# Tiles between the stages of the long transforms: one channel's 32 values side by side instead of 128 channels side by side

## The chip, the cores and the metric

The kernel runs on one core of a Trainium2 chip. The metric is device time in microseconds for one execution; the kernel before was timed three times and the median is used. The engines are called PE (matmul; its weight load is a separate queue), DVE (vector), ACT (scalar), POOL (GpSimd) and SP (issues most transfers).

## The reference

One layer of an encoder block on 2048 tokens of width 1024, all in float32:

```
h = rmsnorm(x);  p = h @ W_in                      # 1024 -> 512 Fourier + 3 x 512 Hyena
y_f = rmsnorm(Re FFT2(positions, 64 channels of a group))     # 8 groups
y_h = rmsnorm(hyena(x1, x2, v)):
    u = short_conv(u)                              # 3 taps
    k = filters(positions)                         # small sine network, 2 orders x 512 channels
    z = v
    for n, gate in enumerate((x1, x2)):
        z = gate * (irfft(rfft(z, 4096) * rfft(k)[n])[:2048] + z * d[n])
x = x + concat(y_f, y_h) @ W_out
x = x + relu(rmsnorm(x) @ W_fc1)^2 @ W_fc2
out = rmsnorm(x)
```

The change concerns only the transforms: the Fourier mixing, the spectra of the filters `k`, and the two rounds of long convolution.

## The kernel before, in words

The program is one instruction stream per engine; the order in the code is, by engine, the order of execution, and engines meet through semaphores that the tile framework sets.

The stages in order: input projection (0 to about 410 us), Fourier mixing together with the generation of the first filters (410 to about 463), spectra of the filters (to about 656), the Hyena rounds (656 to 915), output projection, then the two layers of the MLP.

A transform of length 4096 (or 2048 in the Fourier part) is split in two factors. Positions are held as two digits; the first stage is a matmul over one digit, then a block transpose brings the other digit onto the partitions, and the second stage is a matmul for each of 32 frequencies. The block transpose is DVE's: it turns each 32x32 block, so the 32 values of one channel that lie on the free side go to 32 partitions, and what comes out is again 32 values for each channel. How these 32 values lie in memory is what changes.

*`fourier`.* For 16 groups of 16 channel pairs a matmul of 512 columns (L414) and a transpose into `G` (L415). Then for each of 17 frequencies up to four matmuls of 132 or 124 columns (L429 to L435) read row `f` of `G`. Between the steps of this generator the generation of filters is advanced.

*`filters`.* Eight units, for two orders and four blocks of 128 channels. `generate` makes the filter in eight steps (matmul L483, DVE's product with the decay L487, a split in a high and a low float32r part). `stage1` runs eight times for a unit: three float32r matmuls by `mm3` (L188 to L190) and a transpose into `Gk` (L535). `stage2` runs eight times: four matmuls of 128 columns with `Gk` as the moving operand (L540), a copy by ACT (L543), and every second time a store of the spectrum to DRAM. Steps of `generate` for the unit after next are put in between by the table `GENERATE`. The last units have no generation beside them.

*`hyena`.* Eight blocks, again two orders by four blocks of 128 channels, software-pipelined by hand. For a block:
- `first` (eight times): two matmuls of 256 columns from `zz` (L629), a transpose from PSUM into `G` (L630).
- `second` (eight times): four matmuls of 128 columns from `G` (L636); the product with the spectrum `ks`, which SP loads from DRAM (L615): ACT makes the swapped copy `zs` (L639, L640), DVE multiplies (L642), POOL multiplies (L643), POOL or DVE adds (L644).
- `inverse` (eight times): four matmuls (L652), and ACT's copy of the result into `V` (L653).
- `turn` (eight times): a transpose from `V` into `W` (L659), SBUF to SBUF.
- `gate` (four times): two matmuls of 512 columns on 64 output rows each, from `W` (L665), and DVE's product with the gate into `zz` (L666).

Block `i` runs its `second` while block `i-1` finishes `inverse` and is turned, block `i-2` is gated and block `i+1` does `first`. `LAG`, `TURNS`, `LAST` and `FIRSTS` fix this order.

All matmuls named here, but for those in `mm3`, are plain float32; the profile records each of them as two passes with a weight load each, so counts are twice those of the code. `pa` takes one of eight PSUM banks, each 512 float32 values wide.

Of the kernel before, what the change touches and what calls it, by code (L numbers as in the profile page):

```python
# [10 lines left out]
F32 = mybir.dt.float32  # L11
# [116 lines left out]
P = 128  # L128
# [6 lines left out]
def hybrid_block(ctx: ExitStack, tc: tile.TileContext, A, out):  # L135
    nc = tc.nc
# [27 lines left out]
    def pa(nm):  # L164
        return ps.tile([P, 512], F32, tag="a", name=nm, bufs=8)
# [241 lines left out]

    def fourier(fp, uf, e1f, ffs):
        groups = [(0,)] + [(f, f + 1) for f in range(1, 17, 2)]
        G = fp.tile([P, 32, 256], F32, tag="Gf", name="Gf")  # L410
        ufv = uf.rearrange("p t (b j) -> p t b j", b=2)
        for c in range(16):
            p = pa("pf1")
            nc.tensor.matmul(p, lhsT=e1f, rhs=ufv[:, :, :, 16 * c : 16 * c + 16], start=True, stop=True)  # L414
            nc.vector.transpose(G.rearrange("p f j -> p j f")[:, 16 * c : 16 * c + 16, :], p.rearrange("p (x j) -> p j x", j=16))  # L415
            yield

        def rows(i):

            n, p = len(groups[i]), pa("pf2")  # L420
            neg = fp.tile([P, 2, P], F32, tag="neg", name="neg", bufs=2)[:, 0:n]
            nc.scalar.mul(neg, ffs[i][:, :, 1], -1.0)
            for s, f in enumerate(groups[i]):
                co, si, ns = ffs[i][:, s, 0], ffs[i][:, s, 1], neg[:, s]
                a, b = p[:, 256 * s : 256 * s + 132], p[:, 256 * s + 132 : 256 * s + 256]
                gr, gi = (G[:, j].rearrange("p (c j) -> p c j", c=2) for j in (f, (16 + f) % 32))
                cos, sin = slice(0, 66), slice(66, 128)
                if f % 16 == 0:
                    nc.tensor.matmul(a, lhsT=co, rhs=gr[:, :, cos], start=True, stop=True)  # L429
                    nc.tensor.matmul(b, lhsT=ns, rhs=gr[:, :, sin], start=True, stop=True)  # L430
                else:
                    nc.tensor.matmul(a, lhsT=co, rhs=gr[:, :, cos], start=True, stop=False)
                    nc.tensor.matmul(a, lhsT=si, rhs=gi[:, :, cos], start=False, stop=True)
                    nc.tensor.matmul(b, lhsT=ns, rhs=gr[:, :, sin], start=True, stop=False)
                    nc.tensor.matmul(b, lhsT=co, rhs=gi[:, :, sin], start=False, stop=True)  # L435
            v = p.rearrange("p (s j) -> p s j", s=2)[:, 0:n]
            va = v[:, :, 0:132].rearrange("p s (c j) -> p s c j", c=2)
            sb = fp.tile([P, 2, 2, 62], F32, tag="sb", name="sb", bufs=2)[:, 0:n]
            nc.scalar.copy(sb, v[:, :, 132:256].rearrange("p s (c j) -> p s c j", c=2))

            row = fp.tile([P, 2, 388], F32, tag="row", name="row", bufs=2)[:, 0:n]

            def part(c, w):
                return row[:, :, c : c + 2 * w].rearrange("p s (c j) -> p s c j", c=2)

            nc.vector.tensor_add(part(0, 62), va[:, :, :, 0:62], sb)
            nc.vector.tensor_sub(part(132, 62), va[:, :, :, 0:62], sb)
            for c in (124, 256):
                nc.scalar.copy(part(c, 4), va[:, :, :, 62:66])
            nc.scalar.copy(row[:, :, 264:388], row[:, :, 0:124])  # L450
            nc.sync.dma_start(yfd[:, groups[i][0] : groups[i][0] + n, :], row)

        for i in range(len(groups)):
            rows(i)
            yield


    def filters(ctx, fp, gp, zp, zzs, norms, emb, wo, e1k, f2):
# [5 lines left out]
        class Unit:  # L464
# [62 lines left out]
            def stage1(self, c):  # L527
                if c == 0 and self is units[7]:

                    self.G = fp.tile([P, 32, 128], F32, tag="kh", name="Gk")  # L530
                elif c == 0:
                    self.G = gp.tile([P, 32, 128], F32, tag="Gk", name="Gk")
                p = pa("pk1")
                mm3(p, e1h, e1l, self.k[0][:, c], self.k[1][:, c], True, True)
                nc.vector.transpose(self.G.rearrange("p f c -> p c f")[:, 16 * c : 16 * c + 16, :], p.rearrange("p (l c) -> p c l", c=16))  # L535

            def stage2(self, q):
                p = pa("pk2")
                for j in range(4):
                    nc.tensor.matmul(p[:, 128 * j : 128 * j + 128], lhsT=f2[:, 4 * q + j, :], rhs=self.G[:, 4 * q + j, :], start=True, stop=True)  # L540
                if q % 2 == 0:
                    self.ks = sp.tile([P, 8, 128], F32, tag="ks", name="ks", bufs=3)
                nc.scalar.copy(self.ks[:, 4 * (q % 2) : 4 * (q % 2) + 4, :], p.rearrange("p (f c) -> p f c", f=4))  # L543
                if q % 2:
                    nc.sync.dma_start(kd[self.ct][self.n][:, 4 * q - 4 : 4 * q + 4, :], self.ks)
# [8 lines left out]
        sp = ctx.enter_context(pool("spectra", "right"))  # L554
# [4 lines left out]
        for i, u in enumerate(units):  # L559
# [12 lines left out]
            for q in range(8):  # L572
# [14 lines left out]
                j = 8 * i + q - 50  # L587
# [5 lines left out]
    def hyena(hp, wp, rp, zz, e1, b1, f2, a2, out_weights, out_ahead):  # L593
# [1 line left out]


        def big(nm):
            return (rp if nm == "W" else wp).tile([P, 32, 128], F32, tag=nm, name=nm, bufs=1 if nm == "W" else 2)

        class Block:  # L600
            def __init__(self, n, ct):
# [21 lines left out]
            def first(self, c):  # L623
                if c == 0:
                    self.G = big("G")
                p = pa("pz1")
                lo = 128 * self.ct + 16 * c
                for sp in range(2):
                    nc.tensor.matmul(p[:, 256 * sp : 256 * sp + 256], lhsT=e1[:, sp, :], rhs=zz[:, :, lo : lo + 16], start=True, stop=True)  # L629
                nc.vector.transpose(self.G.rearrange("p f c -> p c f")[:, 16 * c : 16 * c + 16, :], p.rearrange("p (l c) -> p c l", c=16))  # L630

            def second(self, q):
                ks = self.ahead if q == 0 and self.ahead else self.spectrum(q)
                p = pa("pz2")
                for j in range(4):
                    nc.tensor.matmul(p[:, 128 * j : 128 * j + 128], lhsT=f2[:, 4 * q + j, :], rhs=self.G[:, 4 * q + j, :], start=True, stop=True)  # L636
                p3 = p.rearrange("p (f c) -> p f c", f=4)
                zs = hp.tile([P, 4, 128], F32, tag="zs", name="zs", bufs=4)
                nc.scalar.mul(zs[0:64], p3[64:128], -1.0)  # L639
                nc.scalar.copy(zs[64:128], p3[0:64])  # L640
                y = hp.tile([P, 4, 128], F32, tag="y", name="y", bufs=5)
                nc.vector.tensor_mul(y, p3, ks[:, 0])  # L642
                nc.gpsimd.tensor_mul(zs, zs, ks[:, 1])  # L643
                (nc.gpsimd if self is not blocks[7] and q in (0, 1, 2, 3) else nc.vector).tensor_add(y, y, zs)  # L644
                self.y[q] = y

            def inverse(self, q):
                if q == 0:
                    self.V = big("V")
                p = pa("pv")  # L650
                for j in range(4):
                    nc.tensor.matmul(p[:, 128 * j : 128 * j + 128], lhsT=a2[:, 4 * q + j, :], rhs=self.y[q][:, j, :], start=True, stop=True)  # L652
                nc.scalar.copy(self.V[:, 4 * q : 4 * q + 4, :], p.rearrange("p (f c) -> p f c", f=4))  # L653

            def turn(self, c):
                if c == 0:
                    self.W = big("G" if self is blocks[6] else "W")
                c16 = slice(16 * c, 16 * c + 16)
                nc.vector.transpose(self.W.rearrange("p l c -> p c l")[:, c16, :], self.V.rearrange("p f c -> p c f")[:, c16, :])  # L659

            def gate(self, q):
                p = pa("pb")
                for sp in range(2):
                    h = slice(64 * sp, 64 * sp + 64)
                    nc.tensor.matmul(p[h], lhsT=b1[:, h], rhs=self.W[:, 16 * sp + 4 * q : 16 * sp + 4 * q + 4, :], start=True, stop=True)  # L665
                nc.vector.tensor_mul(  # L666
                    zz[:, 4 * q : 4 * q + 4, self.cs], p.rearrange("p (t c) -> p t c", t=4), self.xg[:, 4 * q : 4 * q + 4, :]
                )
# [585 lines left out]
    with pool("ip") as ip, pool("cp1") as cp1:  # L1254
# [4 lines left out]
        uf = zp.tile([P, NT, 512], F32, tag="zz", name="uf")  # L1259
# [26 lines left out]
        e1f, e1k, turn, gy, e1z, wo, emb, f2 = got  # L1286
    norms = early.enter_context(pool("norms", "right")).tile([P, 2, 4, 128], F32, tag="norms", name="norms")
    with pool("filters") as fp:
        zzs = []
        gp = early.enter_context(pool("gk", "right"))  # L1290
# [10 lines left out]
    zz, = zzs  # L1301
    tp = tabs.enter_context(pool("tabs2", "right"))
    a2 = load(tp, "a2", [P, 32, P], A["a2"])
    b1 = load(tp, "b1", [P, P], A["b1"])
    with pool("raws") as rp:
        with pool("wts") as wp:
# [6 lines left out]
            b = {}  # L1313
# [66 lines left out]
```

## Time and profile before

| | |
|---|---|
| median of three runs | 2447.56 us (2445.29 to 2450.56) |
| the profiled execution, its own time | 2447.51 us |
| its span, first to last instruction | 2445.3 us |
| instructions | 30885 |
| mean granted clock of PE | 0.972 |
| block transposes on DVE (L415, L535, L630, L659) | 208, between 0.99 and 1.28 us each |

The groups in the profile are named by line, engine, operation, and the tiles written and read, then the shapes, the count, the total busy time and the mean in ns, and last the idle time of that engine ahead of the group with what ended it. A stretch of the span can be asked for alone. The chain that ended last is followed back from the end of the program; each of its pieces has a start, a length and a name. PE's durations include a modelled end and overlap each other, so how far apart its matmuls start tells more than how long each is.

### The profile page before, as it was taken

Reading aid. Unit: us, or ns where it says so; the run is one execution under the profiler, and the core shown is the slowest. Engines: PE = TensorE matmul, PEld = TensorE weight load, DVE = VectorE, ACT = ScalarE, POOL = GpSimd, SP = SyncE. Lnnn points to the kernel's source line nnn. Section 1 sums busy time; section 2 is a strip of 40 time slices with the busy share of each in tenths; the row PEclk is TensorE's granted clock in tenths of the full one; section 3 lists DMA queues with packets and bytes.
Section 4 is the critical chain, followed back from the end, with each engine's and each line's share of the span. In section 5 each row is a group of like instructions: output and inputs, shape, how many; then the busy total and the mean of one; then the engine's idle time right before and its main releaser. Section 6 shows DMA issues by size and latency. Waiting matters only on the chain.

```text
span 2445.3 us, 30885 instructions
## 1 busy us (share of the span) xinstructions
PE 2273.4 (93%) x10984; PEld 1880.1 (77%) x10984; DVE 1693.9 (69%) x2408; ACT 1104.6 (45%) x1813; POOL 1134.1 (46%) x750
## 2 busy tenths in 40 slices
PE   8998999889798869998999999999979999899997
PEld 6887887788787747886777778888858888688885
DVE  7998445898788896557443435222269999999997
ACT  6554211555254454445544456555523333433333
POOL 3445323666454522215645456555335454445444
PEclk9999999999899989999999999999989999999999
DMA  7435521457587776557766654333394444554411
GB/s 255 172 137 195 194 78 67 150 175 238 166 188 165 171 191 202 168 177 243 241 222 232 227 201 157 116 105 119 100 351 161 164 147 154 206 203 152 147 43 69
DMA packets 259594, 418.85 MB, mean 171 GB/s; under 512 B 15653, under 2 KB 139887, under 8 KB 255089
## 3 DMA queue, kind: packets, MB, share of 16 engines
q1 hardware_dynamic: 256945, 412.45, 52.5%
q10 hardware_dynamic: 2496, 4.45, 0.6%
q8 instruction: 86, 1.41, 0.2%
q14 instruction: 67, 0.55, 0.1%
HBM read 288.16 MB, written 127.11 MB: 170 GB/s over the span
## 4 chain that ended last, share of the span: by engine, by line
PE 54%; DVE 11%; DMA 7%; issue 2%; ACT 2%; SPq 0%; POOL 0%; DVEq 0%; ACTq 0%; POOLq 0%
PE p2u L188 4%; PE p2u L189 4%; PE p2u L190 4%; PE p1u L188 4%; PE p1u L190 4%; PE p1u L189 4%; PE p2v L188 2%; PE p2v L189 2%; PE p2v L190 2%; DMA w<-in_w_fc 2%; PE po L188 2%; PE po L190 2%; PE po L189 2%; DMA td<-w 2%; DVE W L659 2%
## 5 line engine op out<-in xcount | busy, mean ns | idle before, releaser
L188 PE MATMUL p2u<-qbhm,qahm 128*128 128x512 f32 x504 | 198.6, 394 | 19.1 <-DVE acc L1163 19.1
L188 PE MATMUL pu<-wh,xh 128*128 128x512 f32 x512 | 204.5, 401 | 5.4 <-ACT wh L183 5.4
L189 PE MATMUL pu<-wl,xh 128*128 128x512 f32 x512 | 201.5, 394 | 6.5 <-DVE wl L181 3.7
L190 PE MATMUL pu<-wh,xl 128*128 128x512 f32 x512 | 201.3, 393 | 0.0
L189 PE MATMUL p2u<-qblm,qahm 128*128 128x512 f32 x504 | 197.6, 392 | 0.0
L190 PE MATMUL p2u<-qbhm,qalm 128*128 128x512 f32 x504 | 197.1, 392 | 0.0
L1163 DVE TENSOR_TENSOR acc<-acc,p2u 128x512 f32<-128x512 f32 x256 | 165.1, 677 | 10.0 <-PE p2u L190 9.1
L181 POOL TENSOR_TENSOR qblm<-rb,qbhm 128x1024 fp32r<-128x1024 f32 x48 | 142.8, 2976 | 59.6 <-ACT qbhm L180 41.5
L180 ACT CAST qahm<-s 128x1024 fp32r<-128x1024 f32 x64 | 67.4, 1054 | 203.4 <-PE p2u L189 94.2
L181 POOL TENSOR_TENSOR alm<-W,ahm 128x512 fp32r<-128x512 f32 x63 | 87.1, 1383 | 138.1 <-ACT ahm L180 129.3
L945 DVE TENSOR_TENSOR c<-p1v,ku 128x512 f32<-128x512 f32 x64 | 44.1, 689 | 147.9 <-ACT ku L991 114.8
L390 POOL TENSOR_TENSOR acc<-acc,cw 128x512 f32<-128x512 f32 x45 | 59.9, 1330 | 186.1 <-DVE acc L367 183.3
L188 PEld LDWEIGHTS p2u<-qbhm,qahm 128*128 128x128 f32 x504 | 95.5, 189 | 42.9 <-DVE acc L1163 11.9
L180 ACT CAST qahm<-ra 128x1024 fp32r<-128x1024 f32 x46 | 48.5, 1055 | 174.9 <-PE p2v L189 93.5
L1130 POOL TENSOR_TENSOR s<-ra,s 128x1024 f32<-128x1024 f32 x16 | 39.2, 2451 | 185.8 <-DVE qalm L181 185.7
L181 DVE TENSOR_TENSOR qblm<-rb,qbhm 128x1024 fp32r<-128x1024 f32 x62 | 123.1, 1986 | 0.0
L189 PEld LDWEIGHTS pu<-wl,xh 128*128 128x128 f32 x512 | 97.3, 190 | 28.6 <-DVE wl L181 4.1
L188 PEld LDWEIGHTS pu<-wh,xh 128*128 128x128 f32 x512 | 97.1, 190 | 26.8 <-ACT wh L183 6.5
L188 PE MATMUL p1u<-bm,ahm 128*128 128x512 f32 x252 | 102.0, 405 | 16.7 <-ACT ku L991 16.7
L180 ACT CAST qbhm<-rb 128x1024 fp32r<-128x1024 f32 x110 | 115.0, 1047 | 3.6 <-DVE c L951 3.6
L180 ACT CAST ahm<-s 128x512 fp32r<-128x512 f32 x124 | 76.3, 619 | 84.5 <-POOL s L937 32.2
L190 PEld LDWEIGHTS pu<-wh,xl 128*128 128x128 f32 x512 | 97.2, 190 | 20.3
(388 smaller groups left out, 6979.6 us busy)
## 6 DMA issues: line engine op xcount, KB each, us to landing
W<-in_w_fc SPq DMA_DIRECT2D x66, 512.0 KB, 4.4
ks<-spec SPq DMA_DIRECT2D x128, 256.0 KB, 4.8
ra<-ad SPq DMA_DIRECT2D x32, 1024.0 KB, 4.9
rb<-td SPq DMA_DIRECT2D x64, 512.0 KB, 3.6
ad<-c SPq DMA_DIRECT2D x119, 256.0 KB, 4.0
rb<-in_w_fc SPq DMA_DIRECT2D x46, 512.0 KB, 4.0
dec<-in_decay SPq DMA_DIRECT2D x32, 512.0 KB, 4.5
spec<-ks SPq DMA_DIRECT2D x32, 512.0 KB, 2.8
```

The source lines that it names most:

```text
L180: nc.scalar.copy(hi, src)
L181: (eng or nc.vector).tensor_sub(lo, src, hi)
L188: nc.tensor.matmul(o, lhsT=lh, rhs=rh, start=start, stop=False, skip_group_check=more)
L189: nc.tensor.matmul(o, lhsT=lh, rhs=rl, start=False, stop=False, skip_group_check=more)
L190: nc.tensor.matmul(o, lhsT=ll, rhs=rh, start=False, stop=stop, skip_group_check=more)
L390: nc.gpsimd.tensor_add(m1, m1, cw[:, 3, :])
L659: nc.vector.transpose(self.W.rearrange("p l c -> p c l")[:, c16, :], self.V.rearrange("p f c -> p c f")[:, c16, :])
L945: nc.vector.tensor_add(c, p, other)
L1130: G.tensor_sub(s2, a12, s2)
L1163: nc.vector.tensor_add(t, t, p)
```

## The change

The tiles `Gf`, `Gk`, `G`, `V` and `W` hold, on each partition, 32 values for each of 128 (or 256) channels. Before they are `[128, 32, channels]`: all channels of value 0, then all of value 1. Now they are `[128, channels, 32]`: the 32 values of a channel side by side. What follows from it:
- The block transposes write runs; those out of `V` read runs as well.
- In `fourier` and `first` the moving operand of the first-stage matmul is read in another order, so that a channel's values come out side by side in PSUM too: in `fourier` columns run over the channel, then the 32 values; in `first` each of the two matmuls writes 16 of a channel's 32 values. In `stage1` the matmul and its place in PSUM stay, and the transpose reads PSUM with a step as before.
- The matmuls that take one of the 32 values for all channels (`rows`, `stage2`, `second`, `gate`) read their moving operand with a step of 32 values.
- ACT's copy into `V` writes four values of each channel, with a step.

The number of instructions, their sizes, their order and the transfers stay.

```diff
     def fourier(fp, uf, e1f, ffs):
-        G = fp.tile([P, 32, 256], F32, tag="Gf", name="Gf")
-        ufv = uf.rearrange("p t (b j) -> p t b j", b=2)
+        G = fp.tile([P, 256, 32], F32, tag="Gf", name="Gf")
+        ufv = uf.rearrange("p t (b j) -> p j t b", b=2)
         for c in range(16):
             p = pa("pf1")
-            nc.tensor.matmul(p, lhsT=e1f, rhs=ufv[:, :, :, 16 * c : 16 * c + 16], start=True, stop=True)
-            nc.vector.transpose(G.rearrange("p f j -> p j f")[:, 16 * c : 16 * c + 16, :], p.rearrange("p (x j) -> p j x", j=16))
+            nc.tensor.matmul(p, lhsT=e1f, rhs=ufv[:, 16 * c : 16 * c + 16], start=True, stop=True)
+            nc.vector.transpose(G[:, 16 * c : 16 * c + 16, :], p.rearrange("p (j x) -> p j x", j=16))
...
-                gr, gi = (G[:, j].rearrange("p (c j) -> p c j", c=2) for j in (f, (16 + f) % 32))
+                gr, gi = (G[:, :, j].rearrange("p (c j) -> p c j", c=2) for j in (f, (16 + f) % 32))
...
             def stage1(self, c):
-                    self.G = fp.tile([P, 32, 128], F32, tag="kh", name="Gk")
+                    self.G = fp.tile([P, 128, 32], F32, tag="kh", name="Gk")
...
-                nc.vector.transpose(self.G.rearrange("p f c -> p c f")[:, 16 * c : 16 * c + 16, :], p.rearrange("p (l c) -> p c l", c=16))
+                nc.vector.transpose(self.G[:, 16 * c : 16 * c + 16, :], p.rearrange("p (l c) -> p c l", c=16))
             def stage2(self, q):
-                    nc.tensor.matmul(p[...], lhsT=f2[:, 4 * q + j, :], rhs=self.G[:, 4 * q + j, :], start=True, stop=True)
+                    nc.tensor.matmul(p[...], lhsT=f2[:, 4 * q + j, :], rhs=self.G[:, :, 4 * q + j], start=True, stop=True)
...
             def first(self, c):
-                p = pa("pz1")
+                p = pa("pz1").rearrange("p (c l) -> p c l", c=16)
                 for sp in range(2):
-                    nc.tensor.matmul(p[:, 256 * sp : 256 * sp + 256], lhsT=e1[:, sp, :], rhs=zz[:, :, lo : lo + 16], start=True, stop=True)
-                nc.vector.transpose(self.G.rearrange("p f c -> p c f")[:, 16 * c : 16 * c + 16, :], p.rearrange("p (l c) -> p c l", c=16))
+                    rows = zz[:, :, lo : lo + 16].rearrange("p t c -> p c t")
+                    nc.tensor.matmul(p[:, :, 16 * sp : 16 * sp + 16], lhsT=e1[:, sp, :], rhs=rows, start=True, stop=True)
+                nc.vector.transpose(self.G[:, 16 * c : 16 * c + 16, :], p)
             def second(self, q):
-                    nc.tensor.matmul(p[...], lhsT=f2[:, 4 * q + j, :], rhs=self.G[:, 4 * q + j, :], start=True, stop=True)
+                    nc.tensor.matmul(p[...], lhsT=f2[:, 4 * q + j, :], rhs=self.G[:, :, 4 * q + j], start=True, stop=True)
             def inverse(self, q):
-                nc.scalar.copy(self.V[:, 4 * q : 4 * q + 4, :], p.rearrange("p (f c) -> p f c", f=4))
+                nc.scalar.copy(self.V[:, :, 4 * q : 4 * q + 4].rearrange("p c f -> p f c"), p.rearrange("p (f c) -> p f c", f=4))
             def turn(self, c):
-                nc.vector.transpose(self.W.rearrange("p l c -> p c l")[:, c16, :], self.V.rearrange("p f c -> p c f")[:, c16, :])
+                nc.vector.transpose(self.W[:, c16, :], self.V[:, c16, :])
             def gate(self, q):
-                    nc.tensor.matmul(p[h], lhsT=b1[:, h], rhs=self.W[:, 16 * sp + 4 * q : 16 * sp + 4 * q + 4, :], start=True, stop=True)
+                    rows = self.W[:, :, 16 * sp + 4 * q : 16 * sp + 4 * q + 4].rearrange("p c l -> p l c")
+                    nc.tensor.matmul(p[h], lhsT=b1[:, h], rhs=rows, start=True, stop=True)
```

`big`, which makes `G`, `V` and `W`, asks for `[P, 128, 32]` instead of `[P, 32, 128]`.

More of the change, by code (lines that the diff above doesn't have):

```diff
@@ L528, in stage1 @@
                 if c == 0 and self is units[7]:
-                    self.G = fp.tile([P, 32, 128], F32, tag="kh", name="Gk")
+                    self.G = fp.tile([P, 128, 32], F32, tag="kh", name="Gk")
                 elif c == 0:
-                    self.G = gp.tile([P, 32, 128], F32, tag="Gk", name="Gk")
+                    self.G = gp.tile([P, 128, 32], F32, tag="Gk", name="Gk")
                 p = pa("pk1")
                 mm3(p, e1h, e1l, self.k[0][:, c], self.k[1][:, c], True, True)
-                nc.vector.transpose(self.G.rearrange("p f c -> p c f")[:, 16 * c : 16 * c + 16, :], p.rearrange("p (l c) -> p c l", c=16))
+                nc.vector.transpose(self.G[:, 16 * c : 16 * c + 16, :], p.rearrange("p (l c) -> p c l", c=16))
             def stage2(self, q):
@@ L539, in stage2 @@
                 for j in range(4):
-                    nc.tensor.matmul(p[:, 128 * j : 128 * j + 128], lhsT=f2[:, 4 * q + j, :], rhs=self.G[:, 4 * q + j, :], start=True, stop=True)
+                    nc.tensor.matmul(p[:, 128 * j : 128 * j + 128], lhsT=f2[:, 4 * q + j, :], rhs=self.G[:, :, 4 * q + j], start=True, stop=True)
                 if q % 2 == 0:
@@ L597, in big @@
         def big(nm):
-            return (rp if nm == "W" else wp).tile([P, 32, 128], F32, tag=nm, name=nm, bufs=1 if nm == "W" else 2)
+            return (rp if nm == "W" else wp).tile([P, 128, 32], F32, tag=nm, name=nm, bufs=1 if nm == "W" else 2)
         class Block:
@@ L635, in second @@
                 for j in range(4):
-                    nc.tensor.matmul(p[:, 128 * j : 128 * j + 128], lhsT=f2[:, 4 * q + j, :], rhs=self.G[:, 4 * q + j, :], start=True, stop=True)
+                    nc.tensor.matmul(p[:, 128 * j : 128 * j + 128], lhsT=f2[:, 4 * q + j, :], rhs=self.G[:, :, 4 * q + j], start=True, stop=True)
                 p3 = p.rearrange("p (f c) -> p f c", f=4)
```

## The prediction

> **What bounds the kernel now.** The change touches the transforms between the input projection and the output projection, so I looked first at the page's shares, then at a table of stretches, then inside one stretch at the groups of instructions and at the chain that ended last.
>
> ```profile
> PE 2273.4 (93%) x10984; PEld 1880.1 (77%) x10984; DVE 1693.9 (69%) x2408; ACT 1104.6 (45%) x1813; POOL 1134.1 (46%) x750
> PE   8998999889798869998999999999979999899997
> DVE  7998445898788896557443435222269999999997
> ...
> 500.00:620.00 120.00, 105.47 (x747) 97.16 (x746) 107.51 (x160) 65.04 (x123) 74.51 (x63) 0.96 0.65 219
> 620.00:656.00 36.00, 25.89 (x156) 24.16 (x156) 23.60 (x33) 9.09 (x16) 16.45 (x12) 0.81 0.24 96
> 656.00:915.00 259.00, 217.78 (x1417) 183.35 (x1415) 221.89 (x276) 124.49 (x217) 120.47 (x108) 0.95 0.77 183
> 777.00:837.00 60.00, 51.49 (x346) 43.59 (x345) 51.82 (x63) 28.09 (x50) 31.25 (x28) 0.97 0.73 168
> ```
>
> TensorE is busy 93% of the whole, but that is an average. The last four rows are stretches: length, then busy time of PE, PE's weight load, DVE, ACT and POOL, the granted clock, the DMA share and GB/s. In the filter stage (500 to 620) and the Hyena stage (656 to 915) DVE is as busy as PE: 107.5 of 120 and 51.8 of 60. A busy PE here includes overlapped, modelled ends, so PE's real demand is better taken from how fast matmuls follow each other. The groups of DVE in two Hyena blocks (777.6 to 839.1) and pieces of the chain (start, length, what):
>
> ```profile
> L659 DVE STREAM_TRANSPOSE W<-V 128x512 f32<-128x512 f32 x16 | 18.0, 1187 | 1.2 <-ACT V L653 1.2
> L630 DVE STREAM_TRANSPOSE G<-pz 128x512 f32<-128x512 f32 x17 | 17.5, 1046 | 5.4 <-PE pz L629 5.4
> L642 DVE TENSOR_TENSOR y<-pz,ks 128x512 f32<-128x512 f32 x16 | 10.6, 673 | 0.0
> L644 DVE TENSOR_TENSOR y<-y,zs 128x512 f32<-128x512 f32 x8 | 6.3, 788 | 0.4
> L666 DVE TENSOR_TENSOR zz<-pb,xg 128x512 f32<-128x512 f32 x8 | 5.5, 691 | 1.5 <-PE pb L665 1.5
> ...
> 656.97 7.09 DVE G L630 x8
> 665.27 1.73 PE pz L629 x8
> 672.26 0.89 PE pv L652 x8
> 679.32 0.91 PE pz L636 x8
> 695.21 2.06 DVE W L659 x2
> 745.57 3.58 PE pb L665 x16
> 777.60 3.58 PE pb L665 x16
> 807.60 3.58 PE pb L665 x16
> 839.10 3.61 PE pb L665 x16
> ```
>
> One block runs from one gate to the next: 32.0, 30.0 and 31.5 us, mean 31.2. DVE's five groups sum to 57.9 us for two blocks, 29 us for one. PE needs, by pitch (a float32 product is recorded as two passes): 64 passes of L636 and 64 of L652 at 0.112 us each, 14.3 us; 32 passes of L629 at 0.216, 6.9; the gate 3.6. That is 24.9 us. So DVE, with 2 us of gaps, sets the block, and PE stands 6 us below it.
>
> **The change, part by part.** No instruction is added or removed and no DMA, queue or wait moves; 208 transposes, some 1,560 matmul passes and 64 copies change the steps of their addresses.
>
> *Transposes (gain).* Now each writes its 32-value rows with a step of 512 bytes (1,024 in Gf). W<-V reads with that step too; the others read PSUM with a step of 64 bytes. Afterwards W, G and Gf read and write runs; Gk writes runs but still reads PSUM with the step. No transpose on runs is in the trace. The bounds: no gain at all (1.05 and 1.19 us stay), and the fastest 512-element DVE operation of the profile:
>
> ```profile
> L264 DVE TENSOR_SCALAR turn<-turn 128x512 f32<-128x512 f32 x12 | 5.1, 426 | 0.0
> L535 DVE STREAM_TRANSPOSE Gk<-pk 128x512 f32<-128x512 f32 x64 | 62.4, 1056 | 1.1 <-PE pk L190 1.1
> L415 DVE STREAM_TRANSPOSE Gf<-pf x16: 1016/1049/1087, 420.6 to 440.8; 128x512 f32<-128x512 f32 x16
> ```
>
> I take 0.67 us, the row L642, because it is the plain case: 512 values read from PSUM in runs, written in runs. Against 1046 and 1187 ns this frees 8 x 0.38 + 8 x 0.52 = 7.2 us of DVE in a block. For Gk, whose read stays stepped, I take half, 0.19 us each.
>
> [...]
>
> *Strided matmul reads (possible loss).* L636, L540 and L43x will read G with a step of 128 bytes; L665 reads W so; L629 and L414 read zz and uf with steps of 2,048 and 1,024 bytes. Every column is then a separate place. No matmul in the trace reads so: L629 now reads runs of 16 values and its 0.216 us for 256 columns (0.84 ns a column) is no slower than L652's contiguous 128 in 0.111 (0.87). What speaks for a free stride is that these products are the slow kind. The float32r products take half the time a column:
>
> ```profile
> 1259.02 0.39 PE L190 MATMUL p1u<-zf,alm 128*128 128x512 f32 x1
> ...
> 1261.12 0.40 PE L190 MATMUL p1u<-zf,alm 128*128 128x512 f32 x1
> ```
>
> Nine 512-column passes apart, 2.10 us: 0.233 us each, 0.455 ns a column. So a float32 pass asks for values at half the rate that the read path delivers in runs. DVE's stepped operations are slower than those on runs, but by less than double (1.03 us from one transpose W to the next at 695.21, against 0.67 for L642, a fixed part in both); even if a step halves PE's read path, the float32 pass is still just fed, at 0.91 against 0.86 ns. The float32r products of this stage (pk1) keep contiguous reads. I take no loss. A gain is excluded, since no row shows a stepped access quicker than a run. The upper bound is that PE's reads go at DVE's absolute pace, 1.03 us / 512 = 2.0 ns a value.
>
> [...]
>
> *PSUM writes of L629.* Runs of 256 values become runs of 16. Taken at nothing, since ACT's runs of 16 cost nothing beside whole runs:
>
> ```profile
> L180 ACT CAST kh<-kt 128x512 fp32r<-128x512 f32 x48 | 29.5, 617 | 73.1 <-DVE kt L487 73.1
> L180 ACT CAST ahm<-s 128x512 fp32r<-128x512 f32 x124 | 76.3, 619 | 84.5 <-POOL s L937 32.2 <-PE p1m L189 21.2 <-PE p1v L189 18.0
> L653 ACT COPY V<-pv x64: 585/585/587, 673.5 to 895.6; 128x512 f32<-128x512 f32 x64
> DVE W L659 <- ACT V L653: 5.1, 6, 1.9
> ```
>
> The bound is L629 at double, 6.9 us a block on PE.
>
> *ACT's copies into V* (L653) now write single values 128 bytes apart. Between 0 and the 0.38 us by which a stepped DVE transpose exceeds L642; at the upper end ACT has 8 x 0.38 = 3 us more in a block, on 14 us (28.1 in 60). I take 0: ACT stays half idle, and only the last copy ahead of W is waited for (the last row: six times in all), 2 us at most in total if each is 0.38 later.
>
> *What is late next.* With 7.2 us less DVE needs 21.8 us a block, and PE's 24.9 is the longest. DMA comes close: 0.73 of 31 us is 22 us a block for the spectra, and those loads are freed by DVE (first row), so they start earlier too. One already ended a wait on the chain:
>
> ```profile
> SPq L615 <- DVE y L642: 126.1, 42, 8.9
> 849.13 7.57 DMA ks<-spec
> 581.64 0.89 PE pk L483 x8
> 618.79 5.38 DVE Gk L535 x6
> PE pk L540 <- DVE Gk L535: 24.2, 8, 4.6
> ```
>
> *The sum.* A block at PE's 24.9 plus the same 2 us of gaps is 27 us instead of 31.2: 4 us for each of 7 blocks, 28 us. The last eight W stand on the chain with nothing beside them but gates: 8 x 0.52, 4 us. The first eight G do not gain: PE's pitch of 4 x 0.216 = 0.86 us for each equals DVE's 7.09 / 8 = 0.89. Hyena: -32 us. In the filter stage PE's work by pitch (L483 and L540 512 passes each at 0.111, 192 float32r passes at 0.233, the Fourier products 28) is 187 of the 246 us between 410 and 656, and DVE's is 107.5 of 120 in the middle. 64 x 0.19 + 16 x 0.38 = 18 us of DVE go; the waits of L540 for Gk (24.2 us of idle PE) say that about half reaches the end: -9 us, between 0 and -18. Together -41. The profiled execution took 2447.5 us (span 2445.3 and 2.2 around it), which is the median of the runs, 2447.56, so the forecast is 2406. With transposes at 0.43 DVE is no longer near and PE alone without gaps gives 6 x 7 + 6 + 18 = 66 us: 2381. With transposes at 0.85, halfway, DVE needs 25.3 a block like PE, and with gaps and half the other gains it is some 22 us: 2425.
>
> **The rivals.** *Strided matmuls are slower (slower than before).* Place: the passes of L636, L629, L665 and L540. If a value costs twice its 0.86 ns, PE's block grows by 7.2 + 6.9 + 3.6 = 17.7 to 42.6 us; eight blocks 341 plus 20 us of gaps and ends is 361 instead of 259, +102. Filters and Fourier: 187 + 57 + 28 + 25 of gaps = 297 instead of 246, +51. Time 2600. At 2.0 ns a value (2.3 times) it is about 2650. It decides from where PE's block with gaps, 27 + 17.7x, passes 31.2: x = 0.24; with the filter gain, about 0.3. For it: values read and written 512 bytes apart cost DVE 1.5 to 1.8 times the plain operation (1.03 to 1.19 us against 0.67). Against: half the rate is all a float32 pass asks for. [...]
>
> *The transposes do not depend on the step (no change).* Their time could be that of filling and emptying 32x32 blocks. Then DVE keeps its 29 us and the time is 2447. For it: the G family hardly varies (1016 to 1087 in L415) although Gf steps twice as far as Gk. Against: W, with steps on both sides, takes 1187, the others 1046, so the pattern does count.
>
> *PE or the DMA takes the whole place.* If blocks cannot go below 29 us because the bursts of spectra wait (22 us of transfers in four buffers), the Hyena gain is 2 x 7 + 4 and the time 2425; this lies in the forecast's own range.
>
> **How the numbers follow.** Faster for the stated reason: 0.60 (own range 2381 to 2430). Strided matmuls slower by a third or more: 0.27 (2450 to 2650, likeliest 2600). Transposes unchanged, or gain and loss cancelling: 0.13, of which 0.08 within 0.2% (5 us, about what this measurement can tell from no change). Small net gains and losses fill the rest: faster 0.62, same 0.09, slower 0.29. The likeliest is 2406. The slower case is too probable to leave out, so the range goes from 2380 to its value of 2605.
>
> **What would show it.** Transposes L630 and L659 near 0.67 us, Gk between 0.67 and 1.05. The pitch of L636 still 0.112 us a pass, L629 0.216, the gate 3.6 us for 16. Gates 27 us apart, DVE's share in the Hyena stretch down from 0.86 to about 0.75, and PE's idle before L652 smaller. The forecast is wrong if L636's chain pieces for 8 passes are above 1.1 us, if W or G stay above 0.95 us, or if PE's idle moves to waits for the spectra.

## The result, and the profile after

The changed kernel takes 2571.5 us (2568.3 to 2574.5) against 2447.5 for the kernel before: ratio 1.050, 95% interval 1.048 to 1.052, 124 us slower. The first rival came true, not the forecast. The profiled execution has a span of 2566.1 us. First the page: busy time by engine, and the shares of the engines in the chain that ended last.

```profile
PE 2461.5 (96%) x10984; PEld 1972.3 (77%) x10984; DVE 1629.7 (64%) x2408; ACT 1137.4 (44%) x1813; POOL 1133.7 (44%) x750
...
PE 83%; DMA 7%; DVE 7%; ACT 2%; issue 2%; SPq 0%; POOL 0%; ACTq 0%; DVEq 0%; POOLq 0%
```

The same row of the kernel before:

```profile
PE 54%; DVE 11%; DMA 7%; issue 2%; ACT 2%; SPq 0%; POOL 0%; DVEq 0%; ACTq 0%; POOLq 0%
```

DVE's busy time went down by 64 us as meant, PE's went up by 188, and PE's share of the chain rose from 54% to 83%. The lines from 629 on move down by one (L629 is now L630, L636 L637, L659 L660), those of the gate by two (L665 is now L667). The groups of the transposes, of ACT's copy, and of the matmuls that read with a step:

```profile
L631 DVE STREAM_TRANSPOSE G<-pz 128x512 f32<-128x512 f32 x64 | 45.6, 713 | 113.8 <-PE pz L630 113.8
L535 DVE STREAM_TRANSPOSE Gk<-pk 128x512 f32<-128x512 f32 x64 | 43.5, 701 | 8.0 <-PE pk L190 8.0
L660 DVE STREAM_TRANSPOSE W<-V 128x512 f32<-128x512 f32 x56 | 36.1, 679 | 18.8 <-ACT V L654 18.8
L654 ACT COPY V<-pv 128x512 f32<-128x512 f32 x64 | 67.9, 1064 | 44.1 <-PE pv L653 42.8
L637 PE MATMUL pz<-G,f 128*128 128x128 f32 x512 | 123.6, 396 | 0.8 <-DVE G L631 0.8
L630 PE MATMUL pz<-zz,e1z 128*128 128x256 f32 x256 | 117.8, 607 | 0.0
```

All transposes are at 0.68 to 0.71 us, and those into `G` now wait for PE (113.8 us in L631). The chain of the Hyena stage, pieces with start and length:

```profile
789.89 3.46 PE pz L630 x8
793.36 1.76 PE pz L637 x8
824.05 7.00 PE pb L667 x16
866.28 6.99 PE pb L667 x13
908.52 7.00 PE pb L667 x16
```

Before, 8 passes of the second stage took 0.89 us and of the first 1.73, and 16 passes of the gate 3.58; now 1.76, 3.46 and 7.00 (one gate shows 13 records of 16; some are missing in a trace). Each of these matmuls, which read single values, takes twice as long: 1.72 ns a value at a step of 128 bytes (1.76 / 8 / 128), 1.69 at 2,048 (3.46 / 8 / 256). The block goes from 31.2 to 42.2 us (824.05 to 866.28 to 908.52), which is 8 x (1.76 + 0.89) + 4 x 3.46 + 7.0 = 42.0 with nothing between. The stretch of two blocks (length; busy time of PE, its weight load, DVE, ACT, POOL; clock, DMA share, GB/s) says the same:

```profile
824.00:909.00 85.00, 85.00 (x355) 56.16 (x356) 40.99 (x64) 36.63 (x51) 32.04 (x28) 1.00 0.55 124
```

PE never idles and DVE is half idle. Where the 124 us are, by the first start of the first-stage matmul and the last start of the gate product in each stage:

```profile
L629 PE MATMUL pz<-zz,e1z x256: 379/379/634, 655.9 to 856.2; 128*128 128x256 f32 x128
...
L666 DVE TENSOR_TENSOR zz<-pb,xg x32: 660/691/711, 715.0 to 915.7; 128x512 f32<-128x512 f32 x32
```
```profile
L630 PE MATMUL pz<-zz,e1z x256: 590/610/612, 691.4 to 979.2; 128*128 128x256 f32 x128
...
L668 DVE TENSOR_TENSOR zz<-pb,xg x32: 677/691/692, 783.7 to 1038.9; 128x512 f32<-128x512 f32 x32
```

The first pair is of the kernel before, the second of the changed one. The Hyena stage took 259.8 us and takes 347.5, +88; all that lies ahead of it ends 35.5 us later. Together 123, beside 121 by which the spans of these two executions differ.

### The profile page after: what moved, and what is told of

Its sections match the earlier page's. It is cut to its first block, busy times and chain, and to the rows that moved or that the text cites. A ratio compares the mean times of both kernels' runs of the same rounds, so it can differ in the third digit from the quotient of the medians.

```text
span 2566.1 us, 30885 instructions
## 1 busy us (share of the span) xinstructions
PE 2461.5 (96%) x10984; PEld 1972.3 (77%) x10984; DVE 1629.7 (64%) x2408; ACT 1137.4 (44%) x1813; POOL 1133.7 (44%) x750
## 4 chain that ended last, share of the span: by engine, by line
PE 83%; DMA 7%; DVE 7%; ACT 2%; issue 2%; SPq 0%; POOL 0%; ACTq 0%; DVEq 0%; POOLq 0%
PE pk L540 4%; PE pz L630 4%; PE pz L637 4%; PE p2u L188 4%; PE p2u L189 4%; PE p2u L190 4%; PE pu L189 4%; PE pu L190 4%; PE pu L188 4%; PE p1u L188 4%; PE p1u L190 3%; PE p1u L189 3%; PE p2v L188 2%; PE p2v L189 2%; PE p2v L190 2%; PE pv L653 2%
## 5 line engine op out<-in xcount | busy, mean ns | idle before, releaser
L637 PE MATMUL pz<-G,f 128*128 128x128 f32 x512 | 123.6, 396 | 0.8 <-DVE G L631 0.8
L540 PE MATMUL pk<-Gk,f 128*128 128x128 f32 x512 | 118.2, 396 | 6.1 <-DVE Gk L535 6.1
L637 PEld LDWEIGHTS pz<-G,f 128*128 128x128 f32 x512 | 103.4, 206 | 25.8 <-issue 18.6
L631 DVE STREAM_TRANSPOSE G<-pz 128x512 f32<-128x512 f32 x64 | 45.6, 713 | 113.8 <-PE pz L630 113.8
```

The source lines that it names most:

```text
L631: nc.vector.transpose(self.G[:, 16 * c : 16 * c + 16, :], p)
```

## The experiments

**Is it the steps of all these matmuls, and does the step in PSUM count?** In the changed kernel the first-stage matmuls of `first` and `fourier` read runs of 16 again.

```diff
...
-                    rows = zz[:, :, lo : lo + 16].rearrange("p t c -> p c t")
-                    nc.tensor.matmul(p[:, :, 16 * sp : 16 * sp + 16], lhsT=e1[:, sp, :], rhs=rows, start=True, stop=True)
-                nc.vector.transpose(self.G[:, 16 * c : 16 * c + 16, :], p)
+                    nc.tensor.matmul(p[:, 256 * sp : 256 * sp + 256], lhsT=e1[:, sp, :], rhs=zz[:, :, lo : lo + 16], start=True, stop=True)
+                nc.vector.transpose(self.G[:, 16 * c : 16 * c + 16, :], p.rearrange("p (l c) -> p c l", c=16))
```

> The changed kernel, but the first-stage matmuls of first and fourier read zz and uf in runs of 16 again (as before the change), and the transposes after them read PSUM with a step of 64 bytes. Theory A (a matmul that finds each value in another place takes 1.7 ns a value, twice a plain float32 pass; the step in PSUM costs DVE nothing): a block falls from 42.2 to 35.2 us (8 x 4 passes at 0.216 instead of 0.434), Hyena -56 us, Fourier 32 passes at 0.43 instead of 0.87, -14: about 2502 us; transposes into G and Gf stay at 0.72 us. Rival B (the step in PSUM is part of what made the transposes slow): L631 and L415 rise to 0.9 or more; PE still sets the block, so the time is about the same.

Measured 2505.2 us, ratio to before 1.023 (1.021 to 1.025). From the chain and the groups:

```profile
817.07 6.99 PE pb L666 x13
825.15 1.73 PE pz L629 x8
852.34 7.00 PE pb L666 x16
```
```profile
L630 DVE STREAM_TRANSPOSE G<-pz 128x512 f32<-128x512 f32 x64 | 44.7, 706 | 60.2 <-PE pz L629 59.0
```

The block is 35.3 us, L629 is back at 1.73, and the transposes stay at 0.706 though they read PSUM with a step of 64 bytes. So 66 of the 124 us come from the first-stage matmuls, and the step in PSUM costs a transpose nothing (0.706 us with it, 0.713 without); rival B falls. The other 58 stay with the matmuls that still read with a step (the gate at 7.00 for 16 passes), less what DVE gained. In the changed kernel L630 was doubled like L637, whose PSUM writes did not change, so no cost of its PSUM writes in runs of 16 shows beside the read; no run has these writes without the stepped read.

**The same loss without DVE's gain.** The kernel before, with only that matmul of `first` reading with a step:

```diff
...
-                    nc.tensor.matmul(p[:, 256 * sp : 256 * sp + 256], lhsT=e1[:, sp, :], rhs=zz[:, :, lo : lo + 16], start=True, stop=True)
+                    rows = zz[:, :, lo : lo + 16].rearrange("p t c -> p c t")
+                    nc.tensor.matmul(p[:, :, 16 * sp : 16 * sp + 16], lhsT=e1[:, sp, :], rhs=rows, start=True, stop=True)
...
```

> The kernel before, with only the matmul of first (L629) changed: it reads zz with a step of 2048 bytes and its transpose reads PSUM in runs; G is written with the step as before. Theory A: L629 at 0.434 us a pass, PE's block 24.9 + 7.0 = 31.9 us, which passes DVE's 29: with 2 us of gaps 33.9 instead of 31.2, and 7 us more ahead of the first block: about 2447 + 7 x 2.7 + 7 = 2473 us; the transposes into G stay near 1.0 us because it is the step of the write that sets them. Rival B (the step in PSUM set them): transposes at 0.72, which frees DVE 2.6 us a block; PE still sets it, about 2470 us.

Measured 2481.1 us, ratio 1.013 (1.012 to 1.015). Chain, then group:

```profile
766.07 3.58 PE pb L666 x16
795.41 3.46 PE pz L630 x8
799.77 3.58 PE pb L666 x16
```
```profile
L631 DVE STREAM_TRANSPOSE G<-pz 128x512 f32<-128x512 f32 x64 | 67.9, 1061 | 49.4 <-PE pz L630 49.3
```

Blocks 33.7 us apart, as expected; the time is 8 us above the 2473 forecast, and this rest is not traced. The transposes read PSUM in runs and still take 1.06 us (1.05 in the kernel before, with a step): the step of their write to SBUF sets them.

**Two channels side by side.** The tiles of the kernel before in pairs: `[P, 64, 32, 2]`, so that the transposes step 8 bytes and the matmuls read 8 bytes at a place.

```diff
-                nc.vector.transpose(self.G.rearrange("p f c -> p c f")[:, 16 * c : 16 * c + 16, :], p.rearrange("p (l c) -> p c l", c=16))
+                nc.vector.transpose(self.G[:, 8 * c : 8 * c + 8].rearrange("p c f b -> p c b f"), p.rearrange("p (l c b) -> p c b l", c=8, b=2))
...
-                    nc.tensor.matmul(..., rhs=self.G[:, 4 * q + j, :], start=True, stop=True)
+                    nc.tensor.matmul(..., rhs=self.G[:, :, 4 * q + j], start=True, stop=True)
```

`V`, `W` and `Gf` likewise.

> The kernel before, with the tiles between the stages laid out so that two channels lie side by side for each of the 32 values (step of 8 bytes for the transposes and of 256 bytes between pairs of 8 bytes for the matmuls). [...] Rival B (any break in the run costs PE, in proportion to the breaks): passes at 0.165, a block of some 30 us, about 2440 us. Rival C (DVE needs whole runs): transposes stay at 1.05 and 1.19 us, about 2447 us.

Measured 2397.8 us (2392.5 to 2398.6), ratio 0.979 (0.977 to 0.980): this version beats both kernels. Groups and chain:

```profile
L636 PE MATMUL pz<-G,f 128*128 128x128 f32 x512 | 67.7, 273 | 0.8 <-DVE G L630 0.8
L630 DVE STREAM_TRANSPOSE G<-pz 128x512 f32<-128x512 f32 x64 | 44.6, 704 | 18.7 <-PE pz L629 17.4
L653 ACT COPY V<-pv 128x512 f32<-128x512 f32 x64 | 39.1, 611 | 34.9 <-PE pv L652 33.6
L659 DVE STREAM_TRANSPOSE W<-V 128x512 f32<-128x512 f32 x56 | 36.1, 680 | 8.9 <-ACT V L653 8.8
```
```profile
692.88 0.89 PE pz L636 x8
736.20 3.59 PE pb L665 x16
747.82 8.73 DMA ks<-spec
762.61 3.59 PE pb L665 x16
788.62 3.59 PE pb L665 x16
```

Transposes at 0.70 and 0.68, L636 at 0.89 for 8 passes, blocks 26.4 and 26.0 us apart. Both gains are had at once, and rivals B and C fall. The chain of a block now runs through the loads of the spectra (8.73 us of it in one piece).

**Four channels side by side.** The same with `[P, 32, 32, 4]`: the transposes step 16 bytes, the matmuls read 16 bytes at a place (the Fourier tile stays in pairs).

> The kernel before, with four channels side by side for each of the 32 values (two in the Fourier tile): the transposes step 16 bytes, the matmuls read runs of 16 bytes 512 bytes apart. [...] Rival B (DVE's price grows with the distance, 512 bytes being a long step): transposes fall well below 1.0 us, and the time to about 2406 to 2425 us.

Measured 2437.7 us, ratio 0.996 (0.994 to 0.999). The groups:

```profile
L636 PE MATMUL pz<-G,f 128*128 128x128 f32 x512 | 70.6, 283 | 1.5 <-DVE G L630 1.5
L415 DVE STREAM_TRANSPOSE Gf<-pf 128x512 f32<-128x512 f32 x16 | 10.3, 683 | 0.0
L630 DVE STREAM_TRANSPOSE G<-pz 128x512 f32<-128x512 f32 x64 | 67.8, 1094 | 25.1 <-PE pz L629 25.1
L659 DVE STREAM_TRANSPOSE W<-V 128x512 f32<-128x512 f32 x56 | 58.8, 1111 | 4.6 <-ACT V L653 4.6
```

PE keeps its pace (283 ns against 285 before). A step of 16 bytes costs a transpose into `G` as much as one of 512 (1.09 against 1.05 us), and W keeps 1.11 of its 1.19 us: rival B falls. The Fourier transposes, in pairs, went from 1050 to 683 ns, 6 us in all. Pairs are the only one of these layouts that suits both engines.

**Does a stepped read cost DVE too?** The version in pairs, with `V` as before: ACT writes runs, L659 reads with a step of 512 bytes and writes pairs.

```diff
-                nc.vector.transpose(self.W[:, cn].rearrange("p c l b -> p c b l"), self.V[:, cn].rearrange("p c f b -> p c b f"))
+                nc.vector.transpose(self.W[:, cn].rearrange("p c l b -> p c b l"), self.V.rearrange("p f (c b) -> p c b f", b=2)[:, cn])
```

> The version in pairs, but V as in the kernel before: ACT writes V in runs, and the transposes into W read V with a step of 512 bytes and write W in pairs. If the step of the write alone sets a transpose's time (as the step in PSUM cost nothing): L659 stays at 0.68 us and the time at about 2398. If a stepped read of SBUF costs as much as a stepped write: L659 near 1.05 us, 3 us of DVE more in a block whose DVE demand is 22 of 26 us: 2398 to 2408 us. L653 goes back from 611 to 586 ns.

Measured 2407.5 us, ratio 0.981 (0.979 to 0.983), and

```profile
L659 DVE STREAM_TRANSPOSE W<-V 128x512 f32<-128x512 f32 x56 | 57.6, 1065 | 8.2 <-ACT V L653 8.1
```

A stepped read from SBUF costs what a stepped write costs (1.07 us, as against 1.05 for the write into G of the kernel before and 0.68 in pairs on both sides); both together took 1.19.

**Is it a fixed price for each new place, whatever the type?** So far no run spoke against one: float32 singles took 1.7 ns a value, and a pass over 64 pairs took 0.11 us, 1.7 ns a pair. Two runs tried the same on the float32r matmuls of `stage1`, in the kernel before: singles 64 bytes apart, and pairs 64 bytes apart. The edit of the singles:

```diff
-                mm3(p, e1h, e1l, self.k[0][:, c], self.k[1][:, c], True, True)
+                kh, kl = (t[:, c].rearrange("p l j -> p j l") for t in self.k)
+                mm3(p, e1h, e1l, kh, kl, True, True)
...
```

> The kernel before, with only the three float32r matmuls of stage1 changed: they read the filter tile with a step of 64 bytes, one value at a place (their transposes read PSUM in runs and write G with the step as before). [...] Rival B (a stepped read halves the rate of its type): 0.47 us a pass, +45 us of PE work, about 2460 us. Rival C (only the float32 kind suffers): 0.233 us, 2447 us.

> As the run with float32r singles, but the matmuls of stage1 read pairs: 8 bytes at a place, a step of 64 bytes. [...]

Singles 2456.1 us, ratio 1.0017 (1.0002 to 1.0033); pairs 2455.1, 1.0017 (1.0006 to 1.0027). Consecutive passes, by start and modelled length, of the singles and then of the pairs:

```profile
547.18 0.61 PE L189 MATMUL pk<-kl,e1h 128*128 128x512 f32 x1
547.62 0.61 PE L190 MATMUL pk<-kh,e1l 128*128 128x512 f32 x1
```
```profile
542.82 0.61 PE L188 MATMUL pk<-kh,e1h 128*128 128x512 f32 x1
543.25 0.61 PE L189 MATMUL pk<-kl,e1h 128*128 128x512 f32 x1
```

Over more passes than are shown, the singles took 0.433 us a pass, where 512 places at 1.7 ns would be 0.87, and the pairs 0.431. A fixed price for a place falls with the singles (0.85 ns a value, each at a new place). Rival B, that a stepped read halves the rate of its type, comes near for both of these (0.233 us in runs), but not for the float32 pairs, which cost nothing (0.11 us a pass). Two further runs measured the orders of reading one by one, each filter unit with its own order; ACT or DVE put the results back in order. The first read float32r in `stage1`, the second float32 in `stage2`.

> A measurement of the read path alone. The kernel before, but each of the eight filter units reads its 512 float32r values for stage1 (L188 to L190) in another order: steps of 8, 16, 32, 64, 128 and 256 bytes for units 0 to 5, runs of 16 bytes and of 32 bytes with a step of 64 for units 6 and 7; the pitch of each unit's passes is read, runs cost 0.233 us. Singles at 64 bytes took 0.433 and pairs at 64 also 0.433. [...] Theory E (a value that is not followed by its neighbour halves the rate of its type, whatever the step): 0.43 for units 0 to 5, 0.233 for 6 and 7.

> The same for float32. The kernel before, but each of the eight units reads its 128 values for stage2 (L540) in another order: steps of 8, 16, 32, 64, 128 and 256 bytes for units 0 to 5, runs of 8 and of 16 bytes with a step of 64 bytes for units 6 and 7, and ACT puts the result back in order; runs cost 0.111 us a pass. [...] Theory E (a value not followed by its neighbour halves the rate): 0.22 for units 0 to 5, 0.111 for 6 and 7. [...]

One execution each: 2450.2 and 2466.5 us beside 2455.0 for the kernel before. In the float32r run, two passes each with a step of 8 bytes (unit 0), 128 bytes (unit 4), and runs of 16 bytes (unit 6):

```profile
463.74 0.64 PE L190 MATMUL pk<-kh,e1l 128*128 128x512 f32 x1
464.20 0.64 PE L188 MATMUL pk<-kh,e1h 128*128 128x512 f32 x1
...
569.03 0.61 PE L188 MATMUL pk<-k,e1h 128*128 128x512 f32 x1
569.46 0.61 PE L189 MATMUL pk<-k,e1h 128*128 128x512 f32 x1
...
621.94 0.38 PE L188 MATMUL pk<-kh,e1h 128*128 128x512 f32 x1
622.16 0.38 PE L189 MATMUL pk<-kl,e1h 128*128 128x512 f32 x1
```

In the float32 run, 16 passes each with steps of 8, 16, 64, 128 and 256 bytes, and 28 in pairs 64 bytes apart (each length holds one modelled end of some 0.2 us):

```profile
486.58 1.98 PE L546 MATMUL pk<-Gk,f 128*128 128x128 f32 x16
...
514.37 3.79 PE L546 MATMUL pk<-Gk,f 128*128 128x128 f32 x16
...
572.94 3.64 PE L546 MATMUL pk<-Gk,f 128*128 128x128 f32 x16
...
602.25 3.73 PE L546 MATMUL pk<-Gk,f 128*128 128x128 f32 x16
...
631.81 2.35 PE L546 MATMUL pk<-Gk,f 128*128 128x128 f32 x16
...
649.81 3.29 PE L546 MATMUL pk<-Gk,f 128*128 128x128 f32 x28
```

Runs took 1.95 for 16 passes in this view of the kernel before. The orders together, in us a pass:

| order of reading | float32, 128 values | float32r, 512 values |
|---|---|---|
| runs, or 16 bytes at a place | 0.11 | 0.22 to 0.23 |
| pairs at 64 bytes | 0.11 | 0.43 |
| singles, 8 bytes apart | 0.11 | 0.45 |
| singles, 16 to 128 bytes apart | 0.22 to 0.23 | 0.43 to 0.46 |
| singles, 256 bytes apart | 0.14 | 0.49 |

There are only two paces in these rows, full and half of the type's own, but for the last. Where two float32 values lie within 16 bytes (pairs, or a step of 8) the pass keeps its 0.11 us; a float32r pass does not with two (0.43) and does with four (0.22). Theory E holds for float32r within 0.06 us and fails at the float32 step of 8 bytes (0.11 instead of 0.22). Why float32r needs four neighbours where float32 needs two, no run shows. The last row stays open: there, in float32, two places 256 bytes apart alternate, and the pass loses only a quarter (0.14 against 0.11 us).

## Why the prediction was wrong

- **The step that failed** is that of the strided matmul reads: "even if a step halves PE's read path, the float32 pass is still just fed". I took the float32 pass's double time a column as a path half unused. The runs show the opposite: the pass itself is halved, 0.86 to 1.70 ns a value, in every one of the matmuls that the change gave a step (128 to 2,048 bytes). Eight passes of L637 took 1.76 us, above the 1.1 that the prediction named as its sign of being wrong. The step added 8 x 0.87 + 4 x 1.73 + 3.4 = 17.3 us to PE's block, priced at 17.7 in the first rival.
- **The first rival** had the place and the size, and its 2600 was 28 us too high: it added 20 and 25 us of gaps and ends, and a PE that is this late has fewer. In two blocks it has none (85.00 busy of 85.00), and ahead of the Hyena stage its waits for Gk fell from 24.2 to 6.1 us (total, times, longest):

```profile
PE pk L540 <- DVE Gk L535: 6.1, 3, 3.2
```

The Hyena stage came to +88 instead of +102, the stages ahead of it to +35.5 instead of +51. Its point of decision, a third more a value, was passed by far (1.70 instead of 0.86 ns).

- **The transposes** were right: 0.67 us forecast, 0.68 to 0.71 measured. For Gk I took half of the gain because it reads PSUM with a step; it got all (0.70).
- **ACT's copies** were taken at nothing with 0.38 us as the bound; they cost 0.48 (586 to 1064 ns), beyond the bound, and L660 waited 18.8 us for them instead of 5.1. None of these copies stands on the chain of the Hyena stage, where PE is later still. In pairs they cost 0.03 (611 ns).
- **The sum** for DVE's gain is borne out by the version in pairs, which keeps PE's pace: blocks of 26 us where I had 27, and a Hyena stage 32 us shorter, as in the sum (858.6 - 631.2 = 227.4 us against 259.8, by the same two marks):

```profile
L629 PE MATMUL pz<-zz,e1z x256: 377/379/382, 631.2 to 805.2; 128*128 128x256 f32 x128
...
L666 DVE TENSOR_TENSOR zz<-pb,xg x32: 652/692/692, 684.9 to 858.6; 128x512 f32<-128x512 f32 x32
```

What lies ahead of the Hyena stage gained 25 us where I had 9: I gave Gk half its gain and let only half of that time reach the end. This trace is of the fastest execution of the four; by the median the pairs gain 50 us where I had 41. And the loads of the spectra are late next, as the change's last part said.

Two side sums of the prediction are off by their own terms: with transposes at 0.85 us DVE would need 24.7 us a block and not 25.3, and at 2.0 ns a value the first rival comes to some 2670 us and not 2650. Neither enters the forecast.

## What to carry to other kernels

A step that is taken from one engine's access is given to another's, and each has to be priced at the engine that stands behind it: here DVE's 7 us a block were bought with 17 of PE, which had only 6 in hand. Where two engines want opposite layouts, look for a group size that both read at full pace before choosing a side; here pairs of float32 values did, and gave 2%. A resource that no row shows under load is not idle because an instruction is slow: measure the pattern itself, one order for each unit of a loop, before resting a sum on it.

## What the runs showed of the hardware

- A float32 matmul that reads single moving values takes twice its time (0.22 instead of 0.11 us for 128 columns) at the steps tried from 16 to 2,048 bytes but for the one order at 256 (0.14); two values within 16 bytes (8 bytes apart, or a pair) cost nothing (0.11).
- A float32r matmul of 512 columns takes about twice its time on singles and pairs (0.43 to 0.46 instead of 0.23 us; 0.49 with singles 256 bytes apart), while four neighbours together keep it (0.22).
- A DVE block transpose of 128x512 float32 takes 0.68 to 0.71 us on runs or at a step of 8 bytes, 1.05 to 1.11 with an SBUF step of 16, 512 or 1,024 bytes on one side or, at 16, on both, 1.19 to 1.23 with 512 on both; a step of 64 bytes in reading PSUM costs nothing (0.706 against 0.713).
- An ACT copy of 128x512 from PSUM takes 586 ns into runs, 611 into pairs, 1064 into singles 128 bytes apart.
